# Latent attention of layer 1 with transposed scores, and its value products in fp32

## The chip, the core and the metric

One core of a Trainium2 chip runs the whole program. The metric is the device time of one execution in microseconds (us). PE is the matrix engine, PEld its weight loads, DVE the vector engine, ACT the scalar engine, POOL the GpSimd engine, SP the engine that issues most DMAs.

## The reference, cut to what matters

Two layers run over 1024 latent tokens and 256 context tokens. Layer 0 has windowed and neighbourhood attention, layer 1 has latent attention (called C) and differential attention (called D), and each layer ends in a mixture of experts. The change concerns C alone: 8 heads, queries for the 1024 latent tokens, keys and values for all 1280 tokens, 96 numbers per query and key and 64 per value.

```python
def mla_attend(q, k, v):
    s = jnp.einsum('bqhd,bkhd->bhqk', q, k).astype(jnp.float32) * (C_NOPE + C_ROPE) ** -0.5
    p = jax.nn.softmax(s, axis=-1).astype(v.dtype)
    return jnp.einsum('bhqk,bkhd->bqhd', p, v)
```

## The kernel before, in words

Everything is near fp32: a number is split into an f16 high part and an f16 low part, and `K.mm3` (L181 to L185) multiplies two such pairs by three f16 products (high by high, high by low, low by high).

Layer 1's attention is `attn_l1` (L1594). It has eight units: four of C (two heads each, `seq` at L1828) and then four of D (one head each). While a unit's attention runs, the next unit's projection runs beside it: `interleave` (L58) takes steps of the two generators by given weights, and a scheduler below it then fixes each engine's order. The first three C units stand beside `proj_c` of the next C unit, the fourth beside `proj_d` of the first D unit. `proj_c` (L1643) takes ten tiles of 128 tokens: `ps_q` (9 products of 192 columns, eight tiles only) and `ps_kv` (6 of 256 columns), which ACT and DVE read back, split and hand to a DMA transpose (L1673), so that queries and keys stand with their 96 numbers on the partitions. `proj_d` (L1680) has 24 products of 384 columns in each of ten tiles.

Attention of C goes through 16 items a unit (eight query tiles, two heads), in six software stages:

1. `qk` (L1731): scores of 128 queries by 1280 keys into the PSUM tile `S` (three banks, two buffers), as nine products of 512, 512 and 256 columns (S on L183 to L185).
2. `soft` (L1746): DVE takes the row maximum over 1280 columns (L1752) and scales it (L1753). ACT takes the exponential with that bias and sums it (L1755), then writes the f16 high part (L1767).
3. `low` (L1770): DVE or POOL subtracts the high part for the low part (L1774, `K.low_eng` deals them out), and SP issues a DMA transpose of both parts (L1776), 128 by 2560 f16, into the tile `PT1`, with the keys on the partitions.
4. `pv` (L1786), two items later: 30 f16 products of 64 columns into `O` (L183 to L185), then the division and the split for `o_d` (L1812 to L1816, `split_out` at L1779).

D's attention has the same stages with 128-column values and is not changed. `ps_p` (two banks, tag "proj") serves projections and `O` alike.

Of the kernel before, what the change touches and what calls it, by code (L numbers as in the profile page):

```python
# [12 lines left out]
F32 = mybir.dt.float32  # L13
F16 = mybir.dt.float16
# [8 lines left out]
P = 128  # L23
# [9 lines left out]
SW = 256.0  # L33
SP = 1024.0
LNSP = math.log(SP)
ESC = 0.125 / (SA * SA)
UNSC = SA / (SA * SW)

# [1555 lines left out]
def attn_l1(K, moe):  # L1594
    nc, tc = K.nc, K.tc
    with ExitStack() as outer:
# [14 lines left out]
        w_in = K.i["cd_w_in"][0].rearrange("(k p) n -> p k n", p=P)  # L1611
        with ExitStack() as c0:
            latent_l1(K, c0, wk, w_in, hH, hL, cqT, ckT, kr, sub, lc, cos32, sin32)
        ps_s = K.pool("l1pss", 2, PSUM, ctx)
        ps_p = K.pool("l1psp", 2, PSUM, ctx)
        qring = K.pool("l1q", 2, ctx=ctx)
        vring = K.pool("l1v", 2, ctx=ctx)
        pring = K.pool("l1p", 3, ctx=ctx)
        tring = K.pool("l1t", 4, ctx=ctx)
        pctx = ctx.enter_context(ExitStack())  # L1620
        wp = K.pool("l1wp", 2, ctx=pctx, top=True)
        wpc = K.pool("l1wpc", 2, ctx=pctx, top=True)
# [4 lines left out]
        cstg = [wp.tile([P, 2, 2, 2, P], F16, name=f"cstg{i}", bufs=1) for i in range(2)]  # L1627
        for c in cstg:
            nc.gpsimd.memset(c, 0.0)
        units = {}  # L1630

        def load_c(j):
# [10 lines left out]
        def proj_c(j):  # L1643
            (wqh, wql), (wkh, wkl) = load_c(j)
            qk = qring.tile([P, 8, TOK], F16, name="cqk", tag="qk")
            v = vring.tile([P, NT, 2, 128], F16, name="vt1")
            units["c", j] = (qk[:, :4], qk[:, 4:], v)
            for t in range(NT):
                o = slice(t * P, (t + 1) * P)
                stg = cstg[t % 2]  # L1650
                if t < NX:
                    ps = ps_p.tile([P, 2, 96], F32, name="ps_q", tag="proj")
                    for k in range(3):
                        K.mm3(ps.rearrange("p a b -> p (a b)"), cqT[:, k, o], cqT[:, 3 + k, o],
                              wqh[:, k], wql[:, k], k == 0, k == 2)
# [12 lines left out]
                nc.scalar.activation(sk[:, :, 0, :64], kp, AF.Copy, scale=UNSC)  # L1668
                nc.vector.scalar_tensor_tensor(sk[:, :, 1, :64], kp, UNSC, sk[:, :, 0, :64],
                                               op0=ALU.mult, op1=ALU.subtract)  # L1670
                nc.gpsimd.tensor_copy(sk[:, :, :, 64:96], kr[:, t, None].to_broadcast([P, 2, 2, 32]))
                a = 0 if t < NX else 1
                nc.sync.dma_start_transpose(out=qk[:, 4 * a:, o], in_=stg[:, a:].rearrange("p s a b d -> p (s a b d)"))  # L1673
                vt = v[:, t]
                nc.scalar.activation(vt[:, :, :64], vp, AF.Copy, scale=UNSC)
                nc.vector.scalar_tensor_tensor(vt[:, :, 64:], vp, UNSC, vt[:, :, :64],
                                               op0=ALU.mult, op1=ALU.subtract)
                yield

        def proj_d(h):  # L1680
# [41 lines left out]
        SEGS = [(0, 512), (512, 512), (1024, 256)]  # L1722
        esc = {"c": 96.0 ** -0.5 / (SA * SA), "d": ESC}

        def attn(kind, j):
            qT, kT, v = units[kind, j]
            sc = esc[kind]
            f0 = 128 * j + (0 if kind == "c" else 512)
            st = {}

            def qk(it, _):  # L1731
                t, h = it
                S = ps_s.tile([P, 1536], F32, name="S")
                o = slice(t * P, (t + 1) * P)
                for so, m in SEGS:
                    r = slice(so, so + m)
                    if kind == "c":
                        q = [qT[:96, 2 * h + a, o] for a in range(2)]
                        k = [kT[:96, 2 * h + a, r] for a in range(2)]
                        K.mm3(S[:, r], q[0], q[1], k[0], k[1], True, True)  # L1740
                    else:
                        nc.tensor.matmul(S[:, r], qT[:, h, o], kT[:, 2 * h, r], start=True, stop=False)
                        nc.tensor.matmul(S[:, r], qT[:, h, o], kT[:, 2 * h + 1, r], start=False, stop=True)
                return S

            def soft(it, S):  # L1746
                t, h = it
                if h == 0:
                    st[t] = wk.tile([P, 2], F32, name="dd1", bufs=3)
                dd = st[t]  # L1750
                mx = wk.tile([P, 2], F32, name="mx1", bufs=4)
                nc.vector.reduce_max(mx[:, 0:1], S[:, :TOK], axis=AX.X)  # L1752
                nc.vector.tensor_scalar(mx[:, 1:2], mx[:, 0:1], -sc, LNSP, op0=ALU.mult, op1=ALU.add)  # L1753
                Pt = pring.tile([P, TOK], F32, name="Pt1", bufs=3)
                nc.scalar.activation(Pt, S[:, :TOK], AF.Exp, bias=mx[:, 1:2], scale=sc, accum_out=dd[:, h:h + 1])  # L1755
                if kind == "d":
                    if h == 0:
                        st[t, "E0"] = Pt
                        return None
                    E0 = st[t, "E0"]  # L1760
                    rr = wk.tile([P, 2], F32, name="rr1", bufs=4)
                    nc.vector.reciprocal(rr, dd)
                    nc.vector.tensor_mul(rr, rr, lc[:, 4:6])
                    nc.scalar.activation(Pt, Pt, AF.Copy, scale=rr[:, 1:2])
                    nc.vector.scalar_tensor_tensor(Pt, E0, rr[:, 0:1], Pt, op0=ALU.mult, op1=ALU.add)
                Ps = pring.tile([P, 2, TOK], F16, name="Ps1")
                nc.scalar.activation(Ps[:, 0], Pt, AF.Copy)  # L1767
                return Pt, Ps
# [16 lines left out]

            def pv(it, PT):  # L1786
                t, h = it
                if kind == "d":
                    if h == 0:
                        return  # L1790
                    O = ps_p.tile([P, 128], F32, name="O1", tag="proj")
                    for b in range(NT):
                        K.mm3(O, PT[:, b], PT[:, NT + b], v[:, b, :128], v[:, b, 128:], b == 0, b == NT - 1)
                    sq = wk.tile([P, 128], F32, name="osq")
                    ms = wk.tile([P, 1], F32, name="oms")
                    nc.scalar.activation(sq, O, AF.Square, scale=1.0 / (SP * SA * math.sqrt(128.0)), accum_out=ms)
                    K.rsqrt(ms, ms, lc[:, 6:7], wk)
                    of = wk.tile([P, 128], F32, name="of1")
                    nc.vector.scalar_tensor_tensor(of, O, ms, sub, op0=ALU.mult, op1=ALU.mult)
                    split_out(of, t)  # L1800
                    if j == 3:
                        ended.append(t)
                        done.update(ended[:-1])
                    return
                if h == 0:
                    st[t, "O"] = ps_p.tile([P, 2, 64], F32, name="O1", tag="proj")
                O = st[t, "O"]
                for b in range(NT):
                    K.mm3(O[:, h], PT[:, b], PT[:, NT + b], v[:, b, h, :64], v[:, b, h, 64:], b == 0, b == NT - 1)
                if h == 0:  # L1810
                    return
                rr = wk.tile([P, 2], F32, name="rr1", bufs=4)  # L1812
                nc.vector.reciprocal(rr, st[t])
                of = wk.tile([P, 2, 64], F32, name="of2")
                nc.vector.tensor_mul(of, O, rr[:, :, None].to_broadcast([P, 2, 64]))
                split_out(of.rearrange("p a d -> p (a d)"), t)  # L1816

            items = [(t, h) for t in range(NX) for h in range(2)]
            same = lambda i, s: s
# [11 lines left out]
        mix = Mixer(K, 1, big, "hH1", "hL1", ps_p, moe)  # L1831
        for n, (k, j) in enumerate(seq):
            K.low_share = 4 if k == "c" else 10
            gens = [(attn(k, j), 1.6)]
            if n < 7:
                nxt = pj(*seq[n + 1])
                if n == 6:
# [217 lines left out]
```

## Time and profile before

| | us |
|---|---|
| median of 3 runs | 3305.45 |
| lowest, highest | 3302.15, 9118.24 |
| profiled execution, its own time | 3305.77 |
| its span, first to last instruction | 3304.0 |

Times in the rows are counted from the span's start. A row of a group says how often the instruction stands there, how long its engine was busy with it, and the mean of one. A matmul's recorded duration includes its way through the array and overlaps with the next; what it costs in a row of matmuls is the distance from one start to the next. The granted clock is the share of full speed (2.4 GHz) that PE was given; its lower level is 1.2 GHz.

### The profile page before, as it was taken

What the parts mean: (1) busy time and instruction counts of PE and PEld (TensorE: products, weight loads), DVE (VectorE), ACT (ScalarE), POOL (GpSimd) and SP (SyncE); (2) the same over time, 40 slices, a digit from 0 to 9 for tenths busy, and PEclk for the clock granted to TensorE, in tenths of its full rate; (3) what the DMA queues carried; (4) which work ended last, traced back from release to release, by engine and by line L of the source; (5) the groups of instructions that cost most, each with busy time, mean ns of one, the idle gap of its engine ahead of it and who ended that gap; (6) DMA issues with size and microseconds to landing.
All of it is one profiled execution on the core that took longest, in us unless ns stands there. A gap on an engine that the chain in (4) does not pass through costs nothing. (4 is left out here: it accounts for less than half of the span.)

```text
span 3304.0 us, 74455 instructions
## 1 busy us (share of the span) xinstructions
PE 2616.3 (79%) x30127; PEld 1777.7 (54%) x30127; DVE 2599.6 (79%) x4496; ACT 1976.2 (60%) x2949; POOL 1000.7 (30%) x652
## 2 busy tenths in 40 slices
PE   7888889968579989897467777877868579988886
PEld 3545445434267777775245555554534367776662
DVE  6777777778887768887667776778877897889987
ACT  5557777654456656676345655556653565656664
POOL 0123233232342212121432232222221463234443
PEclk8989999979789999999679998999978689999998
DMA  7789898789769889998648999655457589999996
GB/s 238 165 170 190 188 211 186 167 204 221 245 242 336 324 325 367 362 383 328 205 108 148 171 161 183 127 101 101 102 134 201 192 324 343 354 361 379 383 378 255
DMA packets 879159, 790.05 MB, mean 239 GB/s; under 512 B 689397, under 2 KB 719365, under 8 KB 878805
## 3 DMA queue, kind: packets, MB, share of 16 engines
q1 hardware_dynamic: 846981, 714.26, 74.9%
q0 software_dynamic: 26336, 69.85, 6.4%
q8 instruction: 239, 3.92, 0.5%
q10 hardware_dynamic: 5488, 1.09, 0.2%
q14 instruction: 115, 0.94, 0.1%
HBM read 565.85 MB, written 64.55 MB: 191 GB/s over the span
## 5 line engine op out<-in xcount | busy, mean ns | idle before, releaser
L375 DVE SCALAR_TENSOR_TENSOR arena<-arena 128x2048 f16<-128x2048 f32 (+4 forms) x439 | 917.8, 2112 | 175.1 <-ACT arena L374 165.6
L374 ACT ACTIVATE arena<-arena 128x2048 f16<-128x2048 f32 (+4 forms) x439 | 748.7, 1725 | 318.3 <-DMA arena<-in_w_gate_up_dram 195.0
L1364 PE MATMUL pg<-arena 128*128 128x72 f16 (+4 forms) x4736 | 633.3, 210 | 102.8 <-DVE arena L1351 80.4
L1366 PE MATMUL pg<-arena 128*128 128x72 f16 (+4 forms) x4736 | 629.9, 210 | 23.1 <-DVE arena L375 20.3
L1365 PE MATMUL pg<-arena 128*128 128x72 f16 (+4 forms) x4736 | 631.0, 210 | 14.8 <-DVE arena L1351 7.3
L183 PEld LDWEIGHTS <-arena 128*128 128x128 f16 (+1 forms) x3488 | 344.3, 103 | 341.0 <-DMA arena<-arena 128.4
L1365 PEld LDWEIGHTS <-arena 128*128 128x128 f16 x4736 | 473.0, 102 | 69.9 <-issue 66.0
L1366 PEld LDWEIGHTS <-arena 128*128 128x128 f16 x4736 | 472.4, 102 | 52.5 <-DVE arena L375 31.6
L1364 PEld LDWEIGHTS <-arena 128*128 128x128 f16 x4736 | 473.0, 102 | 34.0 <-ACT arena L374 21.4
L184 PEld LDWEIGHTS <-arena 128*128 128x128 f16 (+1 forms) x3488 | 344.3, 103 | 188.0 <-issue 96.2
L1381 POOL DMA_INDIRECT y_d<-arena,rt_sidx x74 | 233.9, 3161 | 615.8 <-ACT arena L1394 310.0
L185 PEld LDWEIGHTS <-arena 128*128 128x128 f16 (+1 forms) x3488 | 344.4, 103 | 129.0 <-issue 22.2
L183 PE MATMUL O<-arena 128*128 128x64 f16 (+1 forms) x1744 | 229.0, 208 | 129.9 <-DMA arena<-arena 98.6
L185 PE MATMUL O<-arena 128*128 128x64 f16 (+1 forms) x1744 | 228.7, 208 | 0.0
L184 PE MATMUL O<-arena 128*128 128x64 f16 (+1 forms) x1744 | 228.4, 208 | 0.0
L1774 POOL TENSOR_TENSOR arena<-arena 128x1280 f16<-128x1280 f32 x57 | 151.6, 2660 | 246.3 <-issue 174.8
L1755 ACT ACTIVATE arena<-S,arena 128x1280 f32<-128x1280 f32 x128 | 169.2, 1322 | 92.8 <-DVE arena L1753 80.6
L1344 POOL DMA_INDIRECT arena<-h_d,rt_gidx x74 | 144.2, 1948 | 233.4 <-PE pt L1350 173.1
L1752 DVE TENSOR_REDUCE arena<-S 128x1 f32<-128x1280 f32 x128 | 189.5, 1482 | 27.4 <-PE S L185 16.6
L195 PE MATMUL py<-arena 128*72 128x512 f16 (+4 forms) x592 | 184.1, 392 | 19.3 <-ACT arena L1376 14.2
L197 PE MATMUL py<-arena 128*72 128x512 f16 (+4 forms) x592 | 182.6, 390 | 0.0
L199 PE MATMUL py<-arena 128*72 128x512 f16 (+4 forms) x592 | 180.6, 386 | 0.0
(390 smaller groups left out, 6262.8 us busy)
## 6 DMA issues: line engine op xcount, KB each, us to landing
arena<-in_w_gate_up_dram SPq DMA_DIRECT2D x256, 1024.0 KB
arena<-in_w_down_dram SPq DMA_DIRECT2D x128, 1024.0 KB
arena<-in_w_ada_dram SPq DMA_DIRECT2D x96, 512.0 KB
arena<-y_d SPq DMA_DIRECT2D x36, 512.0 KB
x_d<-arena POOLq DMA_DIRECT2D x18, 512.0 KB, 3.5
h_d<-arena SPq DMA_DIRECT2D x18, 512.0 KB
arena<-x_d SPq DMA_DIRECT2D x18, 512.0 KB
arena<-in_x_dram SPq DMA_DIRECT2D x16, 512.0 KB
```

Of the source, the lines that this page charges most:

```text
L183: mm(ps, lh, rh, start=first, stop=False)
L184: mm(ps, lh, rl, start=False, stop=False)
L185: mm(ps, ll, rh, start=False, stop=last)
L195: mm(ps[:, o], lh, rh[:, o], start=first, stop=False)
L197: mm(ps[:, o], lh, rl[:, o], start=False, stop=False)
L374: nc.scalar.activation(wh, raw, AF.Copy, scale=scale)
L375: nc.vector.scalar_tensor_tensor(wl, raw, scale, wh, op0=ALU.mult, op1=ALU.subtract)
L1364: mm(pg[:, m, :n], wh, xh, start=k == 0 and m % 4 == 0, stop=False)
L1365: mm(pg[:, m, :n], wh, xl, start=False, stop=False)
L1366: mm(pg[:, m, :n], wl, xh, start=False, stop=k == 7 and m % 4 == 3)
L1381: self.K.nc.gpsimd.indirect_dma_start(out=self.K.y_d[self.l], out_offset=bass.IndirectOffsetOnAxis(ap=sidx, axis=0), in_=y[:n], in_offset= ...
L1752: nc.vector.reduce_max(mx[:, 0:1], S[:, :TOK], axis=AX.X)
```

## The change

C's attention is written anew in `attn_c`, D's keeps the old code as `attn_d`. Scores now stand as [key, query]: a unit is four groups (two halves of 512 queries, two heads) of ten key blocks of 128. For a group, four products of the f16 high parts alone (`maxima`) give the row maxima; `row` turns them by four small products into a row of 512 numbers, which becomes row 96 of the queries; keys have a constant there, so that `scores` (three products of 512 columns, 97 rows deep) subtracts the maximum itself. ACT takes the exponential in fp32, and `pv` multiplies fp32 values (64 columns and a column of ones, for the sum) by the fp32 probabilities, one product of 512 columns a block, into `Oc`. `out` copies the result, transposes it back by four fp32 transposes and divides.

```diff
+MROW = 256.0
...
-        ps_s = K.pool("l1pss", 2, PSUM, ctx)
         ps_p = K.pool("l1psp", 2, PSUM, ctx)
+        psc = ctx.enter_context(ExitStack())
+        ps_s = K.pool("l1psc", 2, PSUM, psc)
+        cwk = K.pool("l1cw", 2, ctx=psc)
...
+        mts = [cwk.tile([P, 4, 97], F16, name=f"mcol{i}", bufs=1) for i in range(2)]
+        for c in mts:
+            nc.gpsimd.memset(c, 0.0)
...
+            nc.vector.memset(c[:, 1, :, 0, 96:97], MROW)
...
-            v = vring.tile([P, NT, 2, 128], F16, name="vt1")
+            v = vring.tile([P, NT, 2, 65], F32, name="vt1")
+            nc.gpsimd.memset(v[:, :, :, 64:], 1.0)
...
-                nc.scalar.activation(vt[:, :, :64], vp, AF.Copy, scale=UNSC)
-                nc.vector.scalar_tensor_tensor(vt[:, :, 64:], vp, UNSC, vt[:, :, :64],
-                                               op0=ALU.mult, op1=ALU.subtract)
+                nc.scalar.activation(v[:, t, :, :64], vp, AF.Copy, scale=UNSC)
...
+        def attn_c(j):
...
+            def maxima(g, a):
+                hf, h = g
+                t = 4 * hf + a
+                S = ps_s.tile([P, 1536], F32, name="S", bufs=1)
+                for so, m in SEGS:
+                    nc.tensor.matmul(S[:, so:so + m], qT[:96, 2 * h, t * P:(t + 1) * P], kT[:96, 2 * h, so:so + m],
+                                     start=True, stop=True)
+                mx = cwk.tile([P, 1], F32, name="mx1", bufs=4)
+                nc.vector.reduce_max(mx, S[:, :TOK], axis=AX.X)
+                nc.vector.tensor_scalar_mul(mts[h][:, a, 96:], mx, -1.0 / MROW)
+
+            def row(g):
+                hf, h = g
+                ps = ps_p.tile([97, 512], F32, name="ps_m", tag="proj")
+                for a in range(4):
+                    nc.tensor.matmul(ps[:, a * P:(a + 1) * P], mts[h][:, a], K.id16, start=True, stop=True)
+                nc.vector.tensor_copy(qT[96:97, 2 * h, hf * 512:hf * 512 + 512], ps[96:97])
+
+            def scores(g, b):
+                hf, h = g
+                St = ps_s.tile([P, 512], F32, name="St")
+                k, q = ([x[:97, 2 * h + a, o] for a in range(2)] for x, o in
+                        ((kT, slice(b * P, (b + 1) * P)), (qT, slice(hf * 512, hf * 512 + 512))))
+                K.mm3(St, k[0], k[1], q[0], q[1], True, True)
+                Pt = cwk.tile([P, 512], F32, name="Pc", bufs=3)
+                nc.scalar.activation(Pt, St, AF.Exp, scale=sc)
+                return Pt
+
+            def pv(g, b, Pt):
+                hf, h = g
+                if b == 0:
+                    O[g] = ps_s.tile([65, 512], F32, name="Oc", bufs=1)
+                nc.tensor.matmul(O[g], v[:, b, h], Pt, start=b == 0, stop=b == NT - 1)
+                if b == NT - 1:
+                    o = outs[g] = cwk.tile([65, 512], F32, name="oc")
+                    nc.scalar.activation(o, O[g], AF.Copy)
+
+            def out(g):
+                hf, h = g
+                ps = ps_p.tile([P, 4, 65], F32, name="ps_o", tag="proj")
+                for a in range(4):
+                    nc.tensor.transpose(ps[:, a], outs[g][:, a * P:(a + 1) * P], K.id32[:65, :65])
...
+            for a in range(4):
+                maxima(groups[0], a)
+                yield
+            row(groups[0])
+            steps = [(g, b) for g in groups for b in range(NT)]
+            late, pts = 2, {}
+            for i in range(len(steps) + late):
+                if i < len(steps):
+                    g, b = steps[i]
+                    n = groups.index(g)
+                    if n < 3 and b % 2 == 0 and b < 8:
+                        maxima(groups[n + 1], b // 2)
+                    if n < 3 and b == 9:
+                        row(groups[n + 1])
+                    pts[i] = scores(g, b)
+                if i >= late:
+                    pv(*steps[i - late], pts.pop(i - late))
+                if i % NT == 5 and i > NT:
+                    out(groups[i // NT - 1])
+                yield
+            out(groups[3])
...
+            if j == 0:
+                psc.close()
+                ps_s = K.pool("l1pss", 2, PSUM, ctx)
+            return attn_d(j)
...
-            gens = [(attn(k, j), 1.6)]
+            gens = [(attn(k, j), 4.4 if k == "c" else 1.6)]
```

On PE before, inside the second C unit: the last f16 score products of one item, and then 30 small value products of an earlier one (`O`), each with a weight load of its own.

```order
L184 LDWEIGHTS arena
L184 MATMUL S<-arena 128x256
L185 LDWEIGHTS arena
L185 MATMUL S<-arena 128x256
L185 LDWEIGHTS arena
L185 MATMUL O_23079<-arena 128x64
L183 LDWEIGHTS arena
L183 MATMUL O_23079<-arena 128x64
```

And on PE in the changed kernel, inside a C unit: a block of scores (`St`, its lines shifted by one), one value product (`Oc`, L1773), and the maxima of the next group (`S`, L1746).

```order
L184 LDWEIGHTS arena
L184 MATMUL St<-arena 128x512
L185 LDWEIGHTS arena
L185 MATMUL St<-arena 128x512
L186 LDWEIGHTS arena
L186 MATMUL St<-arena 128x512
L1773 MATMUL Oc<-arena 65x512
L1746 LDWEIGHTS arena
L1746 MATMUL S<-arena 128x512
```

The 64-column value products are gone; in their place one wide product without a weight load of its own in the program stands behind each block of scores.

On DVE before, at the start of the second C unit, maxima (L1752), their scaling (L1753), the division of an earlier item (L1815, L1782), low parts (L1774) and the projection's work (L433 to L441, L1660) stand in turn.

```order
L1752 TENSOR_REDUCE arena<-S 128x1
L1782 TENSOR_TENSOR arena<-arena 128x128
L1753 TENSOR_SCALAR arena<-arena 128x1
L433 TENSOR_TENSOR arena<-ps_q,arena 128x64
L439 TENSOR_TENSOR arena<-ps_q,arena 128x4x8 x2
L1752 TENSOR_REDUCE arena<-S 128x1
L441 TENSOR_TENSOR arena<-arena 128x64
L1660 SCALAR_TENSOR_TENSOR arena<-ps_q,arena 128x2x64
L1774 TENSOR_TENSOR arena<-arena 128x1280
```

In the changed kernel, at the same place, the last two of the unit's first four maxima (L1749, L1750) and the copy of the finished row (L1757) stand with the projection's work (L434 to L442, L1670) between them.

```order
L1749 TENSOR_REDUCE arena<-S 128x1
L434 TENSOR_TENSOR arena<-ps_q,arena 128x64
L1750 TENSOR_SCALAR arena<-arena 128x1
L440 TENSOR_TENSOR arena<-ps_q,arena 128x4x8 x2
L442 TENSOR_TENSOR arena<-arena 128x64
L1749 TENSOR_REDUCE arena<-S 128x1
L1670 SCALAR_TENSOR_TENSOR arena<-ps_q,arena 128x2x64
L1750 TENSOR_SCALAR arena<-arena 128x1
L1670 SCALAR_TENSOR_TENSOR arena<-arena 128x2x32
L1757 CAST arena<-ps_m 1x512
```

The first exponential of a unit stood behind one maximum; now it stands behind four of them and the copy.

## Rows read from the trace of the kernel before

**Rows 1.** First line of the page: span and instructions.
```profile
span 3304.0 us, 74455 instructions
```

**Rows 2.** Busy time by stretch; a C unit each, from its first exponential.
```profile
core 0: us, PE busy (x) PEld busy (x) DVE busy (x) ACT busy (x) POOL busy (x), PEclk, DMA share, GB/s
1773.00:1846.00 73.00, 55.69 (x662) 38.18 (x662) 57.51 (x123) 49.57 (x89) 23.24 (x22) 0.91 1.01 168
1846.00:1930.00 84.00, 62.02 (x784) 43.34 (x784) 62.76 (x135) 51.61 (x93) 24.72 (x25) 0.92 1.01 171
1930.00:2015.00 85.00, 62.25 (x739) 42.78 (x735) 64.59 (x137) 52.82 (x96) 27.54 (x24) 0.90 0.99 172
2015.00:2112.00 97.00, 83.86 (x892) 53.48 (x892) 71.30 (x141) 54.46 (x88) 21.11 (x14) 0.96 0.86 158
```

**Rows 3.** DMA queues and issues from 1846 to 2015.
```profile
q1 hardware_dynamic: 104837, 27.66, 96.2%
...
arena<-arena SPq DMA_TRANSPOSE x53
```

**Rows 4.** What PE waited for from 1846 to 1930: us, times, longest.
```profile
PE O L183 <- DMA arena<-arena: 10.7, 4, 3.3
PE ps_kv L183 <- DVE arena L1676: 3.8, 2, 2.2
PE S L183 <- ACT arena L1755: 3.1, 7, 1.0
PE ps_kv L183 <- DVE arena L1660: 1.9, 2, 1.4
```

**Rows 5.** PE in order of time, C units: start, duration, engine, line, operation, tiles.
```profile
1943.47 0.38 PE L185 MATMUL S<-arena 96*128 96x512 f16 x1
1943.69 0.27 PE L183 MATMUL S<-arena 96*128 96x256 f16 x1
1943.80 0.27 PE L184 MATMUL S<-arena 96*128 96x256 f16 x1
...
2100.22 0.19 PE L185 MATMUL O<-arena 128*128 128x64 f16 x1
...
2100.48 0.19 PE L185 MATMUL O<-arena 128*128 128x64 f16 x1
2100.51 0.33 PE L183 MATMUL ps_d<-arena 128*128 128x384 f16 x1
2100.67 0.33 PE L184 MATMUL ps_d<-arena 128*128 128x384 f16 x1
```

**Rows 6.** Busy time of the instructions on tile O in the second unit.
```profile
1846.00:1930.00 84.00, 18.63 (x504) 2.24 (x8) 0.00 (x0) 0.92 1.01 171
```

**Rows 7.** Groups by line and shape, final layer norm: fp32 products of 512 columns.
```profile
L1554 PE MATMUL pg<-arena,id 128*128 128x512 f32 x32 | 15.5, 608 | 2.8 <-DMA arena<-y_d 1.9 <-DVE arena L1565 0.7
```

**Rows 8.** The same products in order of time, with their weight loads.
```profile
3256.28 0.19 PEld L1559 LDWEIGHTS pg<-arena 72*128 72x128 f32 x1 [0.24 <-issue]
...
3256.71 3.60 PE L1559 MATMUL pg<-arena 72*128 72x512 f32 x8
```

**Rows 9.** Groups by line and shape from 1846 to 2015.
```profile
L1752 DVE TENSOR_REDUCE arena<-S 128x1 f32<-128x1280 f32 x32 | 47.4, 1481 | 8.6 <-PE S L185 8.5
L1755 ACT ACTIVATE arena<-S,arena 128x1280 f32<-128x1280 f32 x32 | 42.3, 1322 | 12.0 <-DVE arena L1753 12.0
L1774 DVE TENSOR_TENSOR arena<-arena 128x1280 f16<-128x1280 f32 x19 | 34.7, 1826 | 5.7 <-ACT arena L1767 5.7
```

**Rows 10.** Groups by line and shape over the span: 512 columns out of PSUM.
```profile
L706 ACT ACTIVATE arena<-S,arena 128x512 f32<-128x512 f32 x16 | 10.8, 677 | 1.5 <-DVE arena L764 1.1 <-DVE arena L705 0.3
L337 DVE SCALAR_TENSOR_TENSOR arena<-ps_ada,arena 2x512 f32<-2x512 f32 x48 | 32.5, 678 | 5.1 <-PE ps_ada L331 4.3
```

**Rows 11.** In order of time: C's first maximum, D's first exponential.
```profile
1771.23 1.49 DVE L1752 TENSOR_REDUCE arena<-S 128x1 f32<-128x1280 f32 x1
...
2112.42 1.33 ACT L1755 ACTIVATE arena<-S,arena 128x1280 f32<-128x1280 f32 x1 [3.77 <-DVE arena L1753]
```

More of the change, by code (lines that the diff above doesn't have):

```diff
@@ L1613, in attn_l1 @@
             latent_l1(K, c0, wk, w_in, hH, hL, cqT, ckT, kr, sub, lc, cos32, sin32)
-        ps_s = K.pool("l1pss", 2, PSUM, ctx)
         ps_p = K.pool("l1psp", 2, PSUM, ctx)
+        psc = ctx.enter_context(ExitStack())
+        ps_s = K.pool("l1psc", 2, PSUM, psc)
+        cwk = K.pool("l1cw", 2, ctx=psc)
         qring = K.pool("l1q", 2, ctx=ctx)
-        vring = K.pool("l1v", 2, ctx=ctx)
+        vring = K.pool("l1v", 2, ctx=ctx, room={"vt1": 5200})
         pring = K.pool("l1p", 3, ctx=ctx)
         tring = K.pool("l1t", 4, ctx=ctx)
+        mts = [cwk.tile([P, 4, 97], F16, name=f"mcol{i}", bufs=1) for i in range(2)]
+        for c in mts:
+            nc.gpsimd.memset(c, 0.0)
         pctx = ctx.enter_context(ExitStack())
@@ L1673, in proj_c @@
                 nc.sync.dma_start_transpose(out=qk[:, 4 * a:, o], in_=stg[:, a:].rearrange("p s a b d -> p (s a b d)"))
-                vt = v[:, t]
-                nc.scalar.activation(vt[:, :, :64], vp, AF.Copy, scale=UNSC)
-                nc.vector.scalar_tensor_tensor(vt[:, :, 64:], vp, UNSC, vt[:, :, :64],
-                                               op0=ALU.mult, op1=ALU.subtract)
+                nc.scalar.activation(v[:, t, :, :64], vp, AF.Copy, scale=UNSC)
                 yield
@@ L1723, in attn_l1 @@
         esc = {"c": 96.0 ** -0.5 / (SA * SA), "d": ESC}
-        def attn(kind, j):
+        def attn_c(j):
+            qT, kT, v = units["c", j]
+            sc = esc["c"]
+            groups = [(hf, h) for hf in range(2) for h in range(2)]
+            num = lambda hf, h, b=0: 20 * (2 * hf + h) + 2 * b
+            O, outs = {}, {}
+            def maxima(g, a):
[36 more added lines that the diff above has]
+                    nc.tensor.transpose(ps[:, a], outs[g][:, a * P:(a + 1) * P], K.id32[:65, :65])
+                if h == 0:
+                    outs[hf] = cwk.tile([P, 4, 2, 2, 64], F16, name="oc16", bufs=1)
+                os_ = outs[hf]
+                rr = cwk.tile([P, 4, 1], F32, name="rrc")
+                nc.vector.reciprocal(rr, ps[:, :, 64:])
+                of = cwk.tile([P, 4, 64], F32, name="ofc")
+                nc.vector.tensor_mul(of, ps[:, :, :64], rr.to_broadcast([P, 4, 64]))
+                nc.scalar.activation(os_[:, :, 0, h], of, AF.Copy)
+                nc.vector.tensor_sub(os_[:, :, 1, h], of, os_[:, :, 0, h])
+                if h:
+                    for a in range(2):
+                        nc.gpsimd.dma_start(
+                            K.o_d[hf * 512:hf * 512 + 512, a * D + 128 * j:a * D + 128 * j + 128]
+                            .rearrange("(t p) f -> p t f", p=P), os_[:, :, a].rearrange("p t h d -> p t (h d)"))
+            for a in range(4):
[19 more added lines that the diff above has]
+            out(groups[3])
@@ L1726, in attn, with attn_d @@
+        def attn(kind, j):
+            nonlocal ps_s
+            if kind == "c":
+                return attn_c(j)
+            if j == 0:
+                psc.close()
+                ps_s = K.pool("l1pss", 2, PSUM, ctx)
+            return attn_d(j)
+        def attn_d(j, kind="d"):
             qT, kT, v = units[kind, j]
             sc = esc[kind]
-            f0 = 128 * j + (0 if kind == "c" else 512)
+            f0 = 128 * j + 512
             st = {}
@@ L1736, in qk @@
                     r = slice(so, so + m)
[L1737 to L1743, printed above, removed]
+                    nc.tensor.matmul(S[:, r], qT[:, h, o], kT[:, 2 * h, r], start=True, stop=False)
+                    nc.tensor.matmul(S[:, r], qT[:, h, o], kT[:, 2 * h + 1, r], start=False, stop=True)
                 return S
@@ L1755, in soft @@
                 nc.scalar.activation(Pt, S[:, :TOK], AF.Exp, bias=mx[:, 1:2], scale=sc, accum_out=dd[:, h:h + 1])
[L1756 to L1765, printed above, removed]
+                if h == 0:
+                    st[t, "E0"] = Pt
+                    return None
+                E0 = st[t, "E0"]
+                rr = wk.tile([P, 2], F32, name="rr1", bufs=4)
+                nc.vector.reciprocal(rr, dd)
+                nc.vector.tensor_mul(rr, rr, lc[:, 4:6])
+                nc.scalar.activation(Pt, Pt, AF.Copy, scale=rr[:, 1:2])
+                nc.vector.scalar_tensor_tensor(Pt, E0, rr[:, 0:1], Pt, op0=ALU.mult, op1=ALU.add)
                 Ps = pring.tile([P, 2, TOK], F16, name="Ps1")
@@ L1787, in pv @@
                 t, h = it
[L1788 to L1809, printed above, removed]
                 if h == 0:
                     return
-                rr = wk.tile([P, 2], F32, name="rr1", bufs=4)
-                nc.vector.reciprocal(rr, st[t])
-                of = wk.tile([P, 2, 64], F32, name="of2")
@@ L1815, in pv @@
-                nc.vector.tensor_mul(of, O, rr[:, :, None].to_broadcast([P, 2, 64]))
-                split_out(of.rearrange("p a d -> p (a d)"), t)
+                O = ps_p.tile([P, 128], F32, name="O1", tag="proj")
+                for b in range(NT):
+                    K.mm3(O, PT[:, b], PT[:, NT + b], v[:, b, :128], v[:, b, 128:], b == 0, b == NT - 1)
+                sq = wk.tile([P, 128], F32, name="osq")
+                ms = wk.tile([P, 1], F32, name="oms")
+                nc.scalar.activation(sq, O, AF.Square, scale=1.0 / (SP * SA * math.sqrt(128.0)), accum_out=ms)
@@ L1818, in attn @@
+                K.rsqrt(ms, ms, lc[:, 6:7], wk)
+                of = wk.tile([P, 128], F32, name="of1")
+                nc.vector.scalar_tensor_tensor(of, O, ms, sub, op0=ALU.mult, op1=ALU.mult)
+                split_out(of, t)
+                if j == 3:
+                    ended.append(t)
+                    done.update(ended[:-1])
             items = [(t, h) for t in range(NX) for h in range(2)]
```

## Prediction

> **What bounds the kernel now.** I read the busy time by stretch first, then the DMA queues of the same stretch, then what PE waits for, then PE in order of time for the price of one product. The first exponential of C starts at about 1773 and the first of D at 2112.4 [rows 2, 11], so C's four units take 339.4 us of a span of 3304.0 [rows 1]. In the first three units the DMA engines are busy for 0.99 to 1.01 of the time, while PE has 62 of 84 us and DVE 63 [rows 2]. The queue that carries the transposes takes 96.2% of 16 engines, with 53 transposes in 169 us, 32 or 33 of them the probabilities [rows 3]. PE's longest wait in the second unit is for such a transposed tile, 10.7 us, and behind it come waits for DVE and ACT of 3.8, 3.1 and 1.9 us [rows 4]. So these units wait for DMA transposes, and PE has some 22 us of air in each. The fourth unit, beside D's projection, is another matter: DMA 0.86, PE 84 of 97 us. There PE is already nearly the bound.
>
> **The change part by part.** *What goes.* All 64 transposes of probabilities go, and with them the DMA bound: what is left are the projection's transposes, 20 of the 53 in 169 us. DVE loses its low parts, 34.7 us in two units [rows 9], 17 us a unit, POOL its share of them, and ACT the f16 copies. PE loses the 480 products of 64 columns a unit. Their starts lie 0.029 us apart (nine steps from 2100.22 to 2100.48) [rows 5]; with their gaps and slower stretches they keep PE busy for 18.6 us in the second unit [rows 6].
>
> *Scores.* Before, 96 products of 512 columns at 0.215 us (the rows say 0.22, and 0.16 for 384 columns) and 48 of 256 at 0.11 [rows 5]: 25.9 us a unit. Now four groups, ten blocks, three products of 512: 120 x 0.215 = 25.8 us. No difference.
>
> *Maxima.* New on PE: 16 x (2 x 0.215 + 0.11) = 8.6 us a unit. On DVE the reductions stay as they were, 16 of 1.48 us [rows 9].
>
> *Value products.* 40 a unit, fp32, 512 columns. The kernel has such products in its last layer norm: eight tiles by two halves on L1554 are 16 products, and the trace has 32 records [rows 7], two for each. Eight records take 3.60 us, of which the last is about 0.6 long [rows 7, 8], so starts are (3.60 - 0.6) / 7 = 0.43 us apart and a product costs 0.86, as much as four f16 products of that width. 40 x 0.86 = 34.4 us, where 18.6 went.
>
> The weight loads of fp32, 0.19 us each [rows 8], lie within that distance and add nothing while fp32 products follow one another; beside f16 products no row shows them. There they cost from 0 to 0.19 us for each of 320 records, 61 us at most; I take 0, as in the rows. The Trainium skill (TensorE: Matmul & The Clock Gate, section on weight-path perf modes) says that the fast weight load is not used for fp32 weights. By that rule each of them is of the slow kind, and if they stood open the time would be that of a rival below; the trace does not show them open.
>
> *Small products.* 16 of 128 columns at 0.054 (a quarter of 0.215), 0.9 us, and 16 fp32 transposes of 65 columns, from nothing to 2 x 65/512 x 0.43 = 0.11 us each; I take the upper end, 1.8 us.
>
> So PE has 25.8 + 8.6 + 34.4 + 2.7 = 71.5 us a unit for attention, where it had 44.5. The projection beside it is 72 products of 192 columns (0.08, by columns) and 60 of 256, 12.4 us, or 240 of 384 columns at 0.16 [rows 5], 38.4 us. A unit cannot be shorter than 83.9 us, the fourth not shorter than 109.9; the sum is 361.6 us, against the 339.4 that C takes today.
>
> *ACT and DVE.* An exponential of 512 columns out of PSUM takes 0.68 us [rows 10]; 40 are 27 us, where today's exponentials take 21 [rows 9] with the f16 copies on top. It has the time of one value product and the next scores, about 2.2 us, before its own value product is due, so it hides. DVE has 16 reductions and their scaling, 26 us, four row copies at 0.68 (bounded by the two-partition row of 512) [rows 10], and the projection: 62.8 - 23.7 - 17.4 leaves 22 us [rows 2, 9], 2.2 a tile. Some 53 of 90: not the bound.
>
> *The start of a unit* is a new wait. `maxima` has one PSUM buffer, so each of the four must be reduced before the next is filled, and the row copy and the first scores stand behind the last. The order of DVE puts two tiles of projection between them. That is 0.5 + 4 x 1.5 + 2 x 2.2 + 0.7 + about 1 of handing over, 12.6 us, in which PE has five maxima (2.7), two tiles of projection (2.5) and small things (1): it idles some 7 us (0 to 10) in each of units two to four. In the first unit the first reduction cannot come before today's 1771.2 [rows 11], because the last keys arrive then; four reductions with one and a half tiles between them and the copy take 10 us.
>
> *Other stalls.* Today's waits of PE other than for DMA are 8.8 us in a unit [rows 4]. The projection's products stand further apart in the new order, and every exponential has slack; I take 5, from 0 to 8.8.
>
> *The sum.* The first scores start at 1781.2. Unit one has 83.9 - 5.2 (already done) + 5 and ends at 1864.9. Units two and three take 83.9 + 7 + 5 = 95.9 each: 2056.7. Unit four takes 109.9 + 12 = 121.9: 2178.6. D's first exponential follows after six products, a reduction and the scaling, 3.3 us: 2181.9, where it is at 2112.4 now. That is 69.5 us late. From this goes 2.6 us: 90 of C's value products stand behind D's first scores today (90 x 0.029) and would not. The prices are those of the full clock. The granted clock is 0.90 to 0.92 in the first three units and 0.96 in the fourth, where PE is busiest [rows 2]; I take 0.97, since the new units are busier still, which costs 3% of 361.6, 11 us. In all 69.5 - 2.6 + 11 = 78 us. The rest of the program keeps its work and order, so the profiled execution's 3305.8 becomes 3384; that execution lies 0.3 us above the median of the runs, so 3384 stands for the median too.
>
> **The rivals.**
> *PE is packed tightly.* The scheduler fills the starts with projection and the stalls vanish, at full clock. Then C ends at 1781.2 + 78.7 + 2 x 83.9 + 109.9, D's first exponential is at 2140.9, and the time is 3306 + 28.5 - 2.6 = 3332. For it speaks that PE reaches 84 of 97 us today with D's projection beside it; against it that the chain of four maxima is data, not order.
> *It runs heavier.* Stalls of 8.8, starts of 10 and a clock that stays at 0.92 (31 us in place of 11) add 15 + 9 + 20: 3428. The clock of units one to three speaks for it; that it was higher wherever PE had more work speaks against.
> *The weight loads stand open* between f16 products, all 320: 3384 + 61 = 3445. For it: nothing in the trace alternates f16 with wide fp32 products. Against: loads of f16 products are hidden throughout.
> *Not slower: the product takes one record.* If an fp32 product with 65 columns of weights went through PE in one record of 0.43 us, 160 x 0.43 = 69 us would go, and the time would be 3315, as today. From below 0.5 us a product this decides. Against it: 128 and 72 rows deep make no difference today, two records each.
> *The transposes were the bound of something later*, so that their absence pays beyond C. D's units run at other loads, and nothing in C's stretch but the transposes uses that queue heavily [rows 3]. It would have to give 150 us to be faster by 2%.
>
> **How the numbers follow.** About 2%, 66 us, is what a measurement of this kernel can tell from no change: the line is at 3372. My forecast, 3384, has 0.55, with a range of its own of 3360 to 3410, four fifths of it above the line: 0.44 slower, 0.11 the same. Packed 0.23, all the same. Heavier 0.13 and open weight loads 0.04, all slower. One record 0.03, the same. Something later 0.02, faster. That makes 0.61 slower, 0.37 the same, 0.02 faster. The range that should hold the time 8 times in 10 goes from 3340, near the packed case, to 3425, near the heavier one.
>
> **What would show it.** Right: DMA share in C's stretch falls from 1.0 to below 0.5; PE is busy for over 85% of it; the value products of L1773 show two records of about 0.43 us distance; D's first exponential lies near 2182 to 2195; each unit starts with four reductions during which PE has holes. Wrong: starts of the value products 0.43 us apart for a whole product, or their distance beside f16 products clearly over 0.86; PE waiting mostly for ACT's exponentials; a difference that arises after D's first exponential.

## The result, and the profile after

The changed kernel takes 3337.86 us, median of four runs (3334.79 to 3354.14), against 3306.57 for the kernel before: a ratio of 1.0111, 95% interval 1.0077 to 1.0145. The ratio is formed without the one slow run of the kernel before (9118.24), and not from the medians. The changed kernel is slower by some 31 us by the medians, 37 by the ratio. The forecast was 3384, its range 3340 to 3425: the sign and the mechanism hold, the size does not, and the median lies 2 us below the range. It also lies below the forecast's own line for "slower", 3372: 1.1% is what it calls "the same", with a chance of 0.37. The rival "packed tightly" (3332) was nearest.

The profiled execution took 3334.79 us. Its busy time by stretch, cut at the first exponential of each C unit and of D, answers to [rows 2]:

```profile
span 3333.0 us, 71314 instructions
```

```profile
core 0: us, PE busy (x) PEld busy (x) DVE busy (x) ACT busy (x) POOL busy (x), PEclk, DMA share, GB/s
1771.20:1860.30 89.10, 85.88 (x404) 40.89 (x403) 43.78 (x110) 36.30 (x85) 6.10 (x15) 0.98 0.16 32
1860.30:1948.80 88.50, 85.26 (x414) 41.06 (x413) 41.12 (x104) 35.35 (x84) 6.06 (x15) 1.00 0.17 33
1948.80:2045.60 96.80, 90.97 (x423) 43.03 (x422) 47.19 (x108) 38.02 (x85) 5.04 (x11) 0.96 0.29 68
2045.60:2149.80 104.20, 103.52 (x480) 48.57 (x479) 44.22 (x105) 36.72 (x78) 2.25 (x3) 1.00 0.15 33
sum 378.60, PE 365.62 PEld 173.55 DVE 176.31 ACT 146.39 POOL 19.45; mean PE 91.41 PEld 43.39 DVE 44.08 ACT 36.60 POOL 4.86
```

C takes 378.6 us where it took 339.4. The DMA share has fallen from 1.0 to 0.16 to 0.29, DVE, ACT and POOL have all lost work, and PE is busy for 365.6 of 378.6 us, at a granted clock of 0.96 to 1.00 (2.4 GHz nearly throughout). The bound has passed from the DMA engines to PE. The queue of the transposes, by the DMA view of 1860 to 2046, beside [rows 3]:

```profile
q1 hardware_dynamic: 25344, 8.34, 20.7%
...
arena<-arena SPq DMA_TRANSPOSE x20
```

Only the projection's 20 transposes are left. What PE waits for in the second unit (1860 to 1949), beside [rows 4]:

```profile
PE S L1746 <- DVE arena L1749: 2.9, 4, 1.5
PE ps_m L1756 <- DVE arena L1750: 0.2, 1, 0.2
```

Every wait of [rows 4] is gone, 10.7 us for transposes and 8.8 for others. What is left is the maxima's one buffer. Elsewhere PE runs without a hole, as in this stretch in order of time:

```profile
1900.29 0.38 PE L184 MATMUL St<-arena 97*128 97x512 f16 x1
1900.51 0.38 PE L185 MATMUL St<-arena 97*128 97x512 f16 x1
1900.73 0.38 PE L186 MATMUL St<-arena 97*128 97x512 f16 x1
1900.94 1.02 PE L1773 MATMUL Oc<-arena 128*65 128x512 f32 x2
1901.80 0.70 PE L1746 MATMUL S<-arena 96*128 96x512 f16 x3
```

A value product starts 0.21 us after the last f16 product ahead of it, and the next f16 product 0.86 us after that. The weight loads, from the engine's own rows at the same place, show that fp32 costs nothing there:

```profile
1900.73 0.35 PEld L1773 LDWEIGHTS Oc<-arena 128*65 128x65 f32 x2
1901.38 0.10 PEld L1746 LDWEIGHTS <-arena 96*128 96x128 f16 x1 [0.29 <-issue]
```

The pair of fp32 loads takes 0.35 us where one f16 load takes 0.10, and the first starts beside the last score product. They are hidden, against the rival of open loads.

Where the 29.0 us between the two spans arise, in the profiled executions and in a second execution of either kernel (both below):

| part of the span, us | before | after | before again | after again | forecast |
|---|---|---|---|---|---|
| start to C's first exponential | 1773.0 | 1771.2 | 1768.2 | 1785.8 | 1782 |
| C: from there to D's first exponential | 339.4 | 378.6 | 340.7 | 375.8 | 411 |
| D: from its first to its last exponential | 372.0 | 363.6 | 371.9 | 362.6 | 369.4 |
| from there to the end | 819.6 | 819.6 | 817.0 | 820.1 | 819.6 |

C costs 35 to 39 us more, and D gives 8 to 9 back. D's first exponential, looked for near 2182 to 2195, stands at 2149.8. The first row is disturbed by layer 0, which no part of the change touches. One instruction near its end, in order of time, before and after:

```profile
1697.60 0.56 ACT L419 ACTIVATE arena<-ps_xt,arena 128x256 f32<-128x256 f32 x1 [1.40 <-PE ps_xt L417]
```

```profile
1687.19 0.56 ACT L420 ACTIVATE arena<-ps_xt,arena 128x256 f32<-128x256 f32 x1 [1.40 <-PE ps_xt L418]
```

It comes 10.4 us earlier in this execution. In the second execution of the changed kernel it stands at 1697.60 again, so that is a difference between executions and no effect of the change. Counted from this instruction, C's first exponential comes after 75.4 and 76.3 us in the two executions of the kernel before, and after 84.0 and 88.2 in those of the changed one: the first unit starts 8 to 13 us later, where the forecast had 9.

### The profile page after: what moved, and what is told of

It is laid out like the page before. It is cut to its first block, busy times and chain, and to the rows that moved or that the text cites. A ratio compares the mean times of both kernels' runs of the same rounds, so it can differ in the third digit from the quotient of the medians.

```text
span 3333.0 us, 71314 instructions
## 1 busy us (share of the span) xinstructions
PE 2710.2 (81%) x28751; PEld 1769.2 (53%) x28751; DVE 2529.4 (76%) x4387; ACT 1912.9 (57%) x2917; POOL 940.5 (28%) x617
## 4 chain that ended last, share of the span: by engine, by line
PE 16%; DVE 13%; DMA 11%; issue 7%; ACT 4%; POOL 2%; SPq 0%; DVEq 0%; POOLq 0%; ACTq 0%
DMA arena<-in_w_gate_up_dram 5%; PE Oc L1773 4%; DVE arena L376 4%; DMA arena<-arena 2%; DMA arena<-in_w_down_dram 2%; DVE arena L1851 1%; ACT arena L375 1%; PE S L1746 1%; PE St L184 1%; PE St L185 1%; PE St L186 1%; PE ps_d L184 1%; PE ps_d L185 1%; PE ps_d L186 1%; DMA arena<-y_d 1%
## 5 line engine op out<-in xcount | busy, mean ns | idle before, releaser
L184 PEld LDWEIGHTS <-arena 128*128 128x128 f16 (+1 forms) x2816 | 279.5, 102 | 277.7 <-DMA arena<-arena 94.0
L185 PEld LDWEIGHTS <-arena 128*128 128x128 f16 (+1 forms) x2816 | 279.5, 102 | 178.2 <-issue 99.5
L186 PEld LDWEIGHTS <-arena 128*128 128x128 f16 (+1 forms) x2816 | 279.2, 102 | 137.9 <-issue 20.4
L1345 POOL DMA_INDIRECT arena<-h_d,rt_gidx x74 | 170.3, 2302 | 228.7 <-PE pt L1351 183.6
L184 PE MATMUL O<-arena 128*128 128x64 f16 (+1 forms) x1104 | 157.8, 212 | 84.1 <-DMA arena<-arena 67.7
L196 PE MATMUL py<-arena 128*72 128x512 f16 (+4 forms) x592 | 182.5, 389 | 18.8 <-ACT arena L1377 13.7
L1766 ACT ACTIVATE arena<-St 128x512 f32<-128x512 f32 x160 | 95.5, 597 | 144.5 <-PE St L186 144.1
L184 PE MATMUL ps_proj<-arena 128*128 128x384 f16 x480 | 160.4, 335 | 11.4 <-DVE arena L626 3.2
L1773 PE MATMUL Oc<-arena 128*65 128x512 f32 x320 | 162.4, 592 | 1.7 <-ACT arena L1776 1.7
L185 PE MATMUL ps_proj<-arena 128*128 128x384 f16 x480 | 160.3, 334 | 1.0 <-DVE arena L376 1.0
L738 POOL TENSOR_TENSOR arena<-arena 128x640 f16<-128x640 f32 (+4 forms) x64 | 94.3, 1473 | 234.6 <-ACT arena L731 225.9
```

The lines of the kernel that those rows point to most:

```text
L184: mm(ps, lh, rh, start=first, stop=False)
L185: mm(ps, lh, rl, start=False, stop=False)
L186: mm(ps, ll, rh, start=False, stop=last)
L196: mm(ps[:, o], lh, rh[:, o], start=first, stop=False)
L1773: nc.tensor.matmul(O[g], v[:, b, h], Pt, start=b == 0, stop=b == NT - 1)
```

## The experiments

Eight runs followed in two jobs, each beside runs of the kernel before (3302.45 us in the first, 3306.15 in the second).

**Both kernels once more.**

> The kernel before, unchanged, for a second trace. Theory: the 10.5 us by which layer 0 (the same instructions in the same order) ended earlier in the trace of the changed kernel belong to the execution, not to the change; then two executions of the kernel before differ by as much there, some 5 to 10 us by the time that C starts. Rival: it belongs to the program (what it loads and where its code lies), and this execution lies within 2 us of the first trace of before.

> The changed kernel, unchanged, for a second trace. If layer 0's 10.5 us belong to the execution, C starts some 5 to 10 us later than in the first trace of it and the time is 3338 to 3345; if they belong to the program, C starts within 2 us of the first trace. In both cases C's stretch, from the first exponential of C to the first of D, is 378 to 380 us long.

They took 3299.89 and 3346.08 us; their phases stand in the table. C's stretch agrees with the first executions within 3 us (340.7 and 375.8), while the start moved by 5 and 15. The instruction shown above stands 5.7 us earlier in the second execution of the kernel before (1691.94) and 10.4 later in that of the changed one, so the theory holds and the rival falls, though the changed kernel's start moved by more than the 5 to 10 expected and its C was 2 us shorter than 378 to 380. So C's stretch is the measure for what follows, and a single time is good to some 10 us.

**f16 probabilities, two products (f16_probs).** Probabilities and values' high and low parts in f16, two value products a block. The probabilities' low parts are left out.

```diff
-                Pt = cwk.tile([P, 512], F32, name="Pc", bufs=3)
+                Pt = cwk.tile([P, 512], F16, name="Pc", bufs=3)
...
-                nc.tensor.matmul(O[g], v[:, b, h], Pt, start=b == 0, stop=b == NT - 1)
+                nc.tensor.matmul(O[g], v[:, b, h, 0], Pt, start=b == 0, stop=False)
+                nc.tensor.matmul(O[g], v[:, b, h, 1], Pt, start=False, stop=b == NT - 1)
```

> The changed kernel, but ACT writes the probabilities in f16 (their low part is left out), and the values stand as f16 high and low parts, so that a value product is two f16 products of 512 columns (2 x 0.215 us) in place of one fp32 product (2 x 0.43). PE loses 40 x 0.43 = 17.2 us in each of four units. Theory A, PE is the bound of C's stretch and each of its microseconds counts: 3338 - 69 = 3269 us, C's units near 73, 73, 80 and 87 us long. Theory B, the units are set by hand-overs (the four maxima in a chain, the exponentials), and PE's work counts only in part: a gain under 35 us, 3303 or more.

3278.71 us, ratio 0.9932 (0.9904 to 0.9960). C's four units together:

```profile
sum 314.30, PE 300.03 PEld 166.11 DVE 181.46 ACT 145.00 POOL 19.84; mean PE 75.01 PEld 41.53 DVE 45.36 ACT 36.25 POOL 4.96
```

C's stretch is 64.3 us shorter over 160 blocks, or 0.40 us a block, where 2 x 0.215 = 0.43 were taken from PE. The median fell by 59 us, nearer to theory A's 69 than to theory B's 35 at most. Nearly every microsecond taken from PE comes off C's stretch, so PE bounds C and the fp32 product is what it pays for.

**One product (high_only).** The second value product goes too, and with it the values' low parts.

> As the kernel with f16 probabilities, and the low part of the values is left out of the product as well (it is still made): one f16 product of 512 columns a block, 0.215 us in place of 0.86. PE loses 40 x 0.645 = 25.8 us in each unit. Theory A (PE is the bound throughout): 3338 - 103 = 3235 us. If another engine becomes the bound on the way (ACT has some 40 us of a unit, DVE some 50), the gain over the kernel with two products stays below the 34 us that PE loses further.

3246.66 us, a single run.

```profile
1907.80:1983.70 75.90, 69.65 (x389) 38.43 (x388) 48.63 (x118) 38.10 (x86) 5.07 (x11) 0.91 0.38 87
...
sum 286.00, PE 270.28 PEld 150.08 DVE 181.85 ACT 144.23 POOL 19.93; mean PE 67.57 PEld 37.52 DVE 45.46 ACT 36.06 POOL 4.98
```

C's stretch is another 28.3 us shorter, or 0.18 a block for a product of 0.215, less than the 34 us of theory A. No other engine has become the bound: PE is busy for 270.3 of 286.0 us. But its busy time fell by 29.8 us only, at a granted clock down to 0.91 in the third unit, and its holes have grown from 14 to 16 us.

**The maxima of the next unit early (early_maxima).** The first four maxima and the row of a unit are issued in the last group of the unit before, and the next C projection gets the weight 1.45.

```diff
-            for a in range(4):
-                maxima(groups[0], a)
-                yield
-            row(groups[0])
+            if j == 0:
+                for a in range(4):
+                    maxima(groups[0], a)
+                    yield
+                row(groups[0])
...
+                    nx = (groups[n + 1], j) if n < 3 else (groups[0], j + 1) if j < 3 else None
```

> The changed kernel, with the first four maxima and the row of a unit issued in the last group of the unit before, as those of the other groups are. From here on C's stretch is the time from C's first exponential to D's first; in the changed kernel it is 378.6 us, and PE is idle in it for 378.6 - 365.6 = 13 us. Theory: the starts of units two to four are where most of what is left of PE's idle time lies (some 3.5 to 6 us each), so the stretch shortens by 10 to 18 us to 361 to 369 and the time goes to some 3325 where the changed kernel has 3338. Rival: the first chain of maxima is hidden by the projection already, or its work only moves the hole to the projection that must now be ready earlier: the stretch stays within 5 us of 378.6.

3321.85 us, ratio 1.0049 (1.0028 to 1.0070), below the changed kernel's interval (1.0077 to 1.0145). Its busy time by stretch:

```profile
1777.80:1856.70 78.90, 78.90 (x362) 36.39 (x361) 39.33 (x85) 33.69 (x74) 4.01 (x11) 1.00 0.12 25
1856.70:1941.10 84.40, 83.82 (x415) 40.85 (x413) 42.57 (x107) 35.16 (x84) 6.04 (x15) 1.00 0.18 35
1941.10:2025.40 84.30, 83.87 (x413) 40.81 (x412) 46.27 (x111) 38.80 (x90) 5.33 (x12) 1.00 0.36 79
2025.40:2137.60 112.20, 111.65 (x528) 53.25 (x526) 48.26 (x118) 38.29 (x81) 4.48 (x6) 1.00 0.12 26
sum 359.80, PE 358.25 PEld 171.30 DVE 176.42 ACT 145.94 POOL 19.87; mean PE 89.56 PEld 42.82 DVE 44.11 ACT 36.48 POOL 4.97
```

PE is busy for 358.3 of 359.8 us, all at full clock. The stretch is 18.8 us shorter than the changed kernel's, a little more than expected. 11.4 us are idle time, of 13.0, that went with the starts, ACT's copies at the units' ends among them (below). The other 7.4 are PE's own busy time; the clock, 0.96 to 1.00 by unit before and 1.00 in all four now, is a part of it, and the rest was not traced. What the new weight does by itself was not tried. And the floor of the forecast stands here as measured: 83.9 us a unit were worked out, and the second and third take 84.4 and 84.3.

**Both together (f16_early).**

> The f16 probabilities (two f16 value products a block) and the early maxima together. The first alone has 3278.7 us and a stretch of C of 314.3 us, of which PE is busy for 300.0. Theory, that PE alone bounds C now: the holes of some 14 us go, most of them, so the stretch is near 302 to 305 and the time near 3268, a ratio of about 0.990 to the kernel before. Rival: with less work on PE the chain of maxima on DVE and the projection's read-back set the pace, and the time stays at 3279.

3259.38 us, ratio 0.9852 (0.9831 to 0.9874). C's stretch is 296.3, PE busy for 292.7. The stretch is 63.5 us shorter than that of early_maxima, again 0.40 a block. It is also below the 302 to 305 expected: not only did most of the holes go, PE's busy time fell as well, from 300.0 to 292.7, with a granted clock of 0.97 over the stretch without the early maxima and 1.00 with them.

**Half the transposes in the kernel before (half_transposes).** The high part's value product is taken a second time where the low part's stood, so that PE keeps its work; what comes out is not the attention, and the kernel serves for its time alone.

```diff
+                if kind == "c":
+                    nc.sync.dma_start_transpose(out=PT[:, :NT], in_=Ps[:, 0])
+                    return PT
...
-                    K.mm3(O[:, h], PT[:, b], PT[:, NT + b], v[:, b, h, :64], v[:, b, h, 64:], b == 0, b == NT - 1)
+                    for k in range(3):
+                        nc.tensor.matmul(O[:, h], PT[:, b], v[:, b, h, 64 * (k == 1):64 * (k == 1) + 64],
+                                         start=b + k == 0, stop=b == NT - 1 and k == 2)
```

> The kernel before, with only the f16 high part of C's probabilities transposed; the low part is still computed on DVE or POOL, and the 30 value products of an item are kept, on the high part alone, so the low parts of the probabilities are left out of the result. This asks whether C's first three units of before really wait for the DMA transposes. Theory: they do (DMA share 0.99 to 1.01). Without half of the probabilities' bytes a unit falls from 84 us towards PE's 62 to 64 plus its other waits of 8.8, about 71; C's stretch goes from 341 to 300 to 315 and the time to some 3265 to 3275. Rival: the transposes run beside a chain on DVE and ACT that takes just as long: the stretch stays within 8 us of 341 and the time near 3300.

3269.37 us, a single run, with 307.9 for C's stretch, both as the theory had them. Its stretches:

```profile
1770.30:1836.60 66.30, 53.22 (x725) 37.72 (x726) 60.63 (x123) 49.91 (x88) 25.44 (x23) 0.97 0.69 119
1836.60:1910.60 74.00, 59.36 (x764) 41.20 (x761) 60.65 (x136) 50.23 (x93) 25.38 (x24) 0.95 0.69 112
1910.60:1983.80 73.20, 60.03 (x729) 41.61 (x729) 63.37 (x137) 53.50 (x96) 27.55 (x23) 0.93 0.72 139
1983.80:2078.20 94.40, 83.47 (x893) 52.59 (x891) 71.78 (x142) 54.93 (x90) 22.16 (x15) 0.96 0.57 102
sum 307.90, PE 256.10 PEld 173.12 DVE 256.42 ACT 208.57 POOL 100.53; mean PE 64.02 PEld 43.28 DVE 64.10 ACT 52.14 POOL 25.13
```

With PE's and DVE's work kept, the second and third unit fall from 84 and 85 us to 74.0 and 73.2. That is the direct evidence that the transposes bound these units of the kernel before. PE's waits from 1770 to 1984 show what would be next, DVE and ACT:

```profile
PE S L183 <- ACT arena L1755: 14.0, 20, 3.1
PE O L1813 <- DVE arena L1660: 8.3, 6, 2.1
PE O L1813 <- DVE arena L1753: 6.2, 5, 2.0
...
PE O L1813 <- DMA arena<-arena: 2.8, 2, 2.5
```

**One product and early maxima (one_product_early).**

> f16 probabilities, the high parts of the values alone (one f16 value product a block, so the values' low parts are left out), and the early maxima. Without the early maxima it took 3246.7 us with a stretch of C of 286.0, of which PE is busy for 270.3. Theory, that PE alone bounds C: the stretch falls by 10 to 15 us, to 271 to 276, and the time to some 3233. Rival: at 64 to 65 us a unit DVE (43 to 46) and the chain from scores over ACT to the value product are close enough that nothing is gained: 3247.

3224.21 us, ratio 0.9760 (0.9733 to 0.9787): the fastest of all, 82 us below the kernel before. The forecast of 271 to 276 for C's stretch was too high:

```profile
1826.10:1885.30 59.20, 58.16 (x374) 34.36 (x373) 43.87 (x117) 34.93 (x84) 6.08 (x15) 1.00 0.30 50
...
sum 261.40, PE 257.25 PEld 146.04 DVE 180.16 ACT 143.97 POOL 20.03; mean PE 64.31 PEld 36.51 DVE 45.04 ACT 35.99 POOL 5.01
```

The stretch is 24.6 us shorter than without the early maxima: 12 us of holes, and 13 of PE's busy time, which fell from 270.3 to 257.3. The work in the stretch stayed, but for a few products: six of `ps_kv` fewer, three of `ps_d` and four of `S` more. So most of the 13 us is the clock. Its mean over the stretch was 0.96 without the early maxima and is 1.00 with them, and 4% of 286 us are 11 us; this is an estimate, as the two granted clocks are given to a hundredth only.

## Why the prediction was wrong

*What bounds the kernel now.* Right: half_transposes shows it.

*The price of PE's work.* Right. The new units were forecast at 83.9 us of PE and measure 84.3 to 84.4 in early_maxima, once nothing waits. The fp32 product was taken as 2 x 0.43 = 0.86 us, and the trace has 0.86. The Trainium skill (FP8 and Floating Point Precision, section TensorE Precision Notes) says that a true fp32 product goes through the array in four passes. The trace agrees as far as the price goes: 0.86 us is four times 0.215, though in two records. The rival of one record and that of open weight loads have both fallen.

*ACT and DVE.* Right that neither bounds: 36 and 44 us of 89. The exponential measures less than was taken, by the groups from 1860 to 2046:

```profile
L1766 ACT ACTIVATE arena<-St 128x512 f32<-128x512 f32 x81 | 48.3, 597 | 63.8 <-PE St L186 63.6
```

*The start of a unit.* Right as a mechanism, too large in size. 7 us of idle time were forecast for each of three starts; PE's waits over C's whole stretch, 1771 to 2150, hold 8.4 + 0.4 = 8.8 us for the maxima, some 2.9 a start:

```profile
PE S L1746 <- DVE arena L1749: 8.4, 10, 1.5
PE ps_o L1782 <- ACT arena L1776: 2.1, 2, 1.4
PE Oc L1773 <- ACT arena L1776: 1.7, 1, 1.7
PE ps_m L1756 <- DVE arena L1750: 0.4, 2, 0.2
```

The reductions stand 2.3 us apart at the second unit's start:

```profile
1847.97 1.49 DVE L1749 TENSOR_REDUCE arena<-S 128x1 f32<-128x1280 f32 x1 [6.47 <-PE S L1746]
...
1850.25 1.49 DVE L1749 TENSOR_REDUCE arena<-S 128x1 f32<-128x1280 f32 x1
...
1852.74 1.48 DVE L1749 TENSOR_REDUCE arena<-S 128x1 f32<-128x1280 f32 x1
...
1855.01 1.49 DVE L1749 TENSOR_REDUCE arena<-S 128x1 f32<-128x1280 f32 x1
...
1857.49 0.70 DVE L1757 CAST arena<-ps_m 1x512 f16<-1x512 f32 x1 [0.60 <-PE ps_m L1756]
```

From the first reduction to the end of the copy the chain is 10.2 us long, where 12.1 were forecast (12.6 with the products ahead of the first reduction), and the scheduler laid two `ps_q` and two `ps_kv` blocks of products into it.

*Other stalls: the step that failed first.* "I take 5, from 0 to 8.8", in each of four units, was carried over from waits of a unit that was itself bound elsewhere. Measured: 3.8 us in all four together, the waits for ACT's copy of `Oc` in the list above. (The list behind the 8.8 goes on with 1.6, 1.0 and 0.7 us, so the upper end was read too low as well; it made no difference.) In half_transposes, where PE does not become the bound, waits of this kind stayed: 14.0, 8.3 and 6.2 us in three units. Whether they vanished here because PE is the bound, or because DVE and ACT have less to do (DVE 44 of 89 us a unit, where it had 63 of 84), no run separates. The forecast had 3 x 7 + 4 x 5 = 41 us of idle time, the profile has 13.0 (378.6 - 365.6), and so has the second execution (375.8 - 362.8). So 28 of the 32 us missed in C are stalls (16) and starts (12).

*The clock: the step that failed second.* "I take 0.97", 11 us. PE's busy time was 365.6 us and 362.8 in the second execution, against 359.7 worked out at full clock (361.6 - 5.2 + 3.3): 3 to 6 us. The third unit prices it: at a granted clock of 0.96 it took 96.8 us, and in the second execution at 1.00 it took 94.1, with as many products:

```profile
1963.30:2057.40 94.10, 88.32 (x423) 42.12 (x422) 47.01 (x108) 37.99 (x86) 5.04 (x11) 1.00 0.29 68
```

*D's start.* The forecast gave 2.6 us back, for the leftover products alone. D gave 8 to 9. The kernel before has this wait of PE between 2108 and 2135:

```profile
PE O L183 <- DMA arena<-arena: 4.0, 1, 4.0
```

C's last transposed tile held PE up after D had begun, and 30 of the leftover products stood behind it. In half_transposes no wait for a tile of C and no product of C is left behind D's first exponential, and D, from 2078.2 to 2444.7, takes 366.5 us: 5.5 less than before. That is the rival "the bound of something later", with some 5 us where it would have needed 150. The other 3 us in D were not traced.

*The sum.* Set beside the profiled execution, 3382 of span were forecast and 3333 measured. C is 32 us of the 49, D 6, and layer 0's early finish the remaining 11, which the second execution did not have. That the total came so near to the packed case's 3332 is in part luck: in C alone, 379 and 376 us lie between the packed case (2140.9 - 1782 = 359) and the forecast (411). With early_maxima the packed case came true: 359.8.

*The chances.* 0.23 for the packed case was too little. Against it stood that "the chain of four maxima is data, not order"; but PE was idle for only some 3 of the chain's 10.2 us, because the projection filled the rest. What part the new weight of C's steps in `interleave` (4.4) has in that was not tried.

## What to carry to other kernels

Waits seen beside one bound should not be added on top of the next without a reason: here DMA went, PE became the bound, the other engines had slack, and of 20 us of waits assumed 3.8 were left. A forecast for a unit that PE bounds is its PE floor plus the holes that are chains of data, each less the independent work that the scheduler can lay into it. Replacing transposes by fp32 products moves work from the DMA queue to PE, at the price of four f16 products for one. f16 probabilities with early maxima keep the gain of the transposed scores without that price, but they leave the probabilities' low parts out, and the fastest kernel the values' low parts too.

## What the runs showed that was not expected

The granted clock was 0.98 to 1.00 in the units that had nearly no holes, and it lay lower in some that had holes, but not in all: the third unit of the changed kernel had 5.8 us of them in both executions, and 0.96 in one and 1.00 in the other. In the second unit's start of the changed kernel PE waited 1.52 us and then ran on at half pace:

```profile
1856.56 0.79 PE L1746 MATMUL S<-arena 96*128 96x512 f16 x2 [1.52 <-DVE arena L1749]
...
1858.74 0.63 PE L184 MATMUL St<-arena 97*128 97x512 f16 x1
1859.17 0.63 PE L185 MATMUL St<-arena 97*128 97x512 f16 x1
1859.59 0.63 PE L186 MATMUL St<-arena 97*128 97x512 f16 x1
1860.02 0.49 PE L184 MATMUL St<-arena 97*128 97x512 f16 x1
```

Score products stand 0.43 us apart, twice their usual 0.215, until 1860. A hole can so cost more than itself. Layer 0, untouched, ended up to 10 us apart between executions, a third of the effect looked for; the phases had to be compared one by one.
